# A hybrid attention and recurrence layer on one Trainium2 core: the two token tiles of a block share one matmul per level of the recurrence

## The chip, the core and the metric

The kernel runs on one core of a Trainium2 chip. A core has a matmul engine (TensorE, PE in the profile, with PEld its weight loads), a vector engine (VectorE, DVE), a scalar engine (ScalarE, ACT), GpSimd (POOL) and SyncE (SP), which issues the DMAs. SBUF is the on-chip memory of 128 partitions, PSUM the memory that matmuls write. Each engine works through its own queue in order, and they wait for each other at semaphores. The metric is the time of one execution on the device in microseconds; lower is better.

## What is computed

One layer for 2048 tokens of width 1024, all in 32-bit floats. The part that the change touches is the token mixer: differential attention (four heads, chunk-causal with chunks of 64 tokens) beside a gated recurrence (four heads, key width 128).

```python
h = _rmsnorm(x, ln1_w[l])
proj = h @ w_in[l]
dq, dk, dv, hq, hf, hi, hg = jnp.split(proj, offs, axis=-1)
...
f = lb + (1.0 - lb) * jax.nn.sigmoid(f_logit.astype(f32))
log_f = jnp.log(f)
k = 1.0 - f
...
def step(state, xs):
    qc, kc, vc, gc = xs
    b = jnp.cumsum(gc, axis=-2)
    rel = jnp.where(causal[:, :, None],
                    b[:, :, :, None, :] - b[:, :, None, :, :], -jnp.inf)
    att = jnp.einsum('bhtk,bhsk,bhtsk->bhts', qc, kc, jnp.exp(rel))
    o = (jnp.einsum('bhts,bhsv->bhtv', att, vc)
         + jnp.einsum('bhtk,bhkv->bhtv', qc * jnp.exp(b), state))
...
x = x + jnp.concatenate([o_diff, o_hgrn], axis=-1) @ w_out[l]
x = x + _conv_ffn(_rmsnorm(x, ln2_w[l]), w_up[l], conv_w[l], conv_b[l], w_down[l])
```

## The kernel before

The program has four stages: the mixer, the out-projection, the up-projection of the feed-forward part and its down-projection. Stages keep their tiles in pools of their own, which are opened when a stage is set up and take the place of the pools of the stage before; a tile that lies where an older one lay waits until the older one has been read for the last time.

**The mixer.** An outer loop runs over four slices `s` (one head of each kind; `WA`, `WB`, `WC` are the weights of a slice, loaded and split into a high and a low part). Inside, a loop over eight blocks `b` of 256 tokens runs the steps of a string of letters (`ORDER`, line 860 and following): projections (`proj_a`, `proj_b`, `proj_c`), transposes, scores and softmax (`attn`), the weighted sum (`attn_o`), the recurrence (`hgrn`) and its output (`hgrn_o`). A block is two tiles of 128 tokens, `j` or `g` = 0 and 1. In the first slice `phase1` (line 210) also normalizes x, transposes it and writes `hT` to memory, for the later slices. The string is only the order of the program text: the scheduler of the programming layer places each engine's instructions, so that projection and score matmuls stand between the matmuls of the recurrence.

**The recurrence**, `hgrn` (line 422). The decay within a tile is built up over seven levels, h = 1, 2, 4 to 64. At a level the queries in the second half of each group of 2h tokens meet the keys in the first half. For each of the two tiles `g`, a matmul of all keys of the tile (128 - h columns of weights) against 64 columns of queries writes half of the tile `lt` (one PSUM buffer, shared with `op` and `sp` of `hgrn_o`); the entries that belong together are copied under the mask `lmask` into `att`. Then the queries `qP` and the keys `kS` are multiplied in place by the decay of their group, and the decays `T` are multiplied pairwise for the next level:

```python
for g in range(2):
    PE.matmul(lt[0:nk, g]..., lhsT=kS[:, g * P:g * P + nk], rhs=qv[:, g * ng:(g + 1) * ng, 1, :], ...)
for g in range(2):
    DVE.copy_predicated(out=att[g][0:nk]..., mask=lmask[0:nk, li]..., data=lt[0:nk, g]...)
DVE.tensor_tensor(out=qv[:, :, 1, :], ...)
DVE.tensor_tensor(out=kvw[:, :, 0, :], ...)
```

`hgrn_o` (line 452) multiplies `att` with the values, adds the part of the running state, normalizes and gates, and writes the rows of the tile to `o_d`. `lmask` and three `att` tiles lie in pools that stay open through all stages; they are made once in `load_rest`, on GpSimd.

**The out-projection** loads eight weight tiles `wo0` to `wo7`, casts each to its high part on ScalarE (line 532) and subtracts for the low part on GpSimd or VectorE (line 533). `load_o` reads a tile of `o_d` back, transposes it and splits it into `oT`; the matmuls `pjo` (lines 594 to 596) go through the eight weight tiles in turn, three passes each.

Of the kernel before, what the change touches and what calls it, by code (L numbers as in the profile page):

```python
# [8 lines left out]
F32 = mybir.dt.float32  # L9
F32R = mybir.dt.float32r  # L10
BF16 = mybir.dt.bfloat16
U8 = mybir.dt.uint8
# [13 lines left out]
TOP, FEW, SMALL, SMALL2 = 480, 192, 320, 192  # L26
# [14 lines left out]
class Rows:  # L41
# [16 lines left out]
    def small(self, shape, dt, **kw):  # L58
        return self.pool.tile(shape, dt, **kw)


@with_exitstack
def hymba_kernel(ctx, tc, x, ln1_w, w_in, q_norm_w, k_norm_w, lam_q1, lam_k1, lam_q2, lam_k2,
# [54 lines left out]
    lmask = few.tile([P, 7, 64], U8, name="lmask")  # L118
    NATT = 3
    atts = [cst.tile([P, P], F32, name=f"att{n}") for n in range(NATT)]  # L120

# [13 lines left out]
    def load_rest(tmp, tmq):  # L135
        lamv = tmp[:, 0:256].rearrange("p (n e) -> p n e", n=4)
        lbd = tmp[:, 256:268].rearrange("p (n e) -> p n e", n=3)
        lmf = tmq[:, 0:448].rearrange("p (l e) -> p l e", l=7)
# [27 lines left out]
        for li, h in enumerate(LEVELS):  # L166
            v = lmf[:, li, :].rearrange("p (n h) -> p n h", h=h)
            n = 64 // h
            for pat, base, mul in (([-2 * h, n], 0, 1), ([2 * h, n], h - 1, -1)):
                POOL.affine_select(out=v, in_=v, pattern=[pat, [0, h]], compare_op=ALU.is_ge,  # L170
                                   fill=0.0, base=base, channel_multiplier=mul)
        POOL.tensor_copy(out=lmask, in_=lmf)
        for a in atts:
            POOL.memset(a, 0.0)
# [10 lines left out]
    with ExitStack() as ms:  # L185
        wp = pool(ms, "wp", 1)
# [26 lines left out]
        def phase1(b):  # L213
# [17 lines left out]
            for d0 in range(0, ND, 2):  # L231
# [4 lines left out]
                for dd in range(2):  # L236
                    dt = d0 + dd
                    ACT.activation(out=hT[:, 0, dt, :], in_=tp[:, dd, :], func=AF.Copy, scale=ln1c[:, dt:dt + 1])
                    DVE.scalar_tensor_tensor(out=hT[:, 1, dt, :], in0=tp[:, dd, :], scalar=ln1c[:, dt:dt + 1],  # L239
                                             in1=hT[:, 0, dt, :].bitcast(F32), op0=ALU.mult, op1=ALU.subtract)  # L240
# [15 lines left out]
        for s in range(4):  # L256
# [82 lines left out]
            def attn(b, j):  # L339
# [9 lines left out]
                for si, (k0, k1) in enumerate(segs):  # L349
                    for c in range(2):  # L350
# [8 lines left out]
                        if last:  # L359
                            DVE.memset(sc[0:64, w - 64:w], -3.0e38)  # L360
# [61 lines left out]
            def hgrn(b):  # L422
# [4 lines left out]
                att = [atts[(2 * b + g) % NATT] for g in range(2)]  # L427
                for li, h in enumerate(LEVELS):
                    nb = BLK // (2 * h)
                    nk = P - h  # L430
                    lt = ps.tile([P, 2, 64], F32, name="lt", tag=HT, bufs=HB)
                    qv = qP.rearrange("p (n two h) -> p n two h", two=2, h=h)
                    kvw = kS.rearrange("p (n two h) -> p n two h", two=2, h=h)
                    for g in range(2):
                        ng = nb // 2
# [468 lines left out]
```

## Time and profile before

| | us |
|---|---|
| median of 3 runs | 2775.85 (2774.70 to 2777.01) |
| the profiled execution | 2776.42 |
| its span, first to last instruction | 2774.7 |
| TensorE busy in the span | 2676.6 (96%) |
| VectorE busy | 1904.0 (69%) |
| ScalarE busy | 1201.2 (43%) |
| GpSimd busy | 1074.5 (39%) |

The mixer takes the first 45% of the span; the out-projection follows to about 1400 us, the up-projection to about 2100, the down-projection to the end. How the rows further down are to be read: in the timeline the first number is the start in us, the second how long the instruction (or the xN like it, merged) took, then engine, line, operation, out<-in by the program's names and the shapes; in brackets stands the idle time of the engine before it and what ended it. Matmuls overlap, so what one takes from its engine is the distance to the start of the next. A 32-bit matmul is two passes and shows as two instructions. In the table by stretch there are, for each stretch, its length and the busy time (with the number of instructions) of PE, PEld, DVE, ACT and POOL, then the granted share of TensorE's clock, the DMA share and GB/s. In the groups by line and shape: line, engine, operation, names, shapes, count, then busy us and mean ns of one, then idle time before them. In the list of waits: engine and tile that waited, for whom, us in total, times, longest.

### The profile page before, as it was taken

How to read it: one execution, taken by the hardware profiler on the slowest of the kernel's cores; microseconds unless marked ns; L12 is line 12 of the kernel's file. 1: busy time of each engine (PE TensorE's matmuls, PEld its weight loads, DVE VectorE, ACT ScalarE, POOL GpSimd, SP SyncE). 2: the span in 40 equal slices, each digit the busy share in tenths (PEclk: the TensorE clock that was granted, in tenths of full speed). 3: DMA queues.
4: the chain of work that ended last, by engine and by line, in shares of the span. 5: the costliest groups of instructions: out<-in, count | busy, mean ns of one | idle time of the engine just before them, and what ended most of it. 6: DMA issues, size and time to landing. Idle time of an engine off the chain costs nothing. (4 is left out here: it accounts for less than half of the span.)

```text
span 2774.7 us, 42676 instructions
## 1 busy us (share of the span) xinstructions
PE 2676.6 (96%) x15298; PEld 2342.9 (84%) x15298; DVE 1904.0 (69%) x3987; ACT 1201.2 (43%) x2814; POOL 1074.5 (39%) x1153
## 2 busy tenths in 40 slices
PE   7999999999999999989999999999999998899999
PEld 6998999999999999978887888887888886687887
DVE  5677855676567656673328666668777778977787
ACT  4555543454345434443334443445334344434332
POOL 3332222222222222121325434433343346887775
PEclk9999999999999999999999999999999999999999
DMA  5222311131211311124764222225222234775754
GB/s 187 100 84 98 121 68 69 69 122 65 73 68 59 107 69 69 39 80 155 237 204 144 92 76 84 91 76 183 76 91 81 80 91 122 166 163 132 180 169 170
DMA packets 236627, 306.15 MB, mean 110 GB/s; under 512 B 15374, under 2 KB 202110, under 8 KB 232318
## 3 DMA queue, kind: packets, MB, share of 16 engines
q1 hardware_dynamic: 229502, 278.25, 30.3%
q0 software_dynamic: 6912, 25.17, 5.3%
q8 instruction: 121, 1.98, 0.3%
q14 instruction: 92, 0.75, 0.1%
HBM read 198.50 MB, written 104.86 MB: 109 GB/s over the span
## 5 line engine op out<-in xcount | busy, mean ns | idle before, releaser
L679 PE MATMUL q<-xT,WS 128*128 128x512 f32 x704 | 274.3, 390 | 2.8 <-DVE xT L612 2.7
L678 PE MATMUL q<-xT,WS 128*128 128x512 f32 x704 | 274.0, 389 | 2.5 <-ACT xT L611 2.5
L680 PE MATMUL q<-xT,WS 128*128 128x512 f32 x704 | 274.2, 389 | 0.0
L792 PE MATMUL pd<-TW,SG 128*128 128x512 f32 x616 | 245.4, 399 | 19.9 <-DVE acc L798 6.5
L794 PE MATMUL pd<-TW,SG 128*128 128x512 f32 x616 | 242.3, 394 | 3.3 <-DVE SG L612 3.3
L793 PE MATMUL pd<-TW,SG 128*128 128x512 f32 x616 | 243.6, 396 | 1.0 <-DVE TW L612 1.0
L611 ACT CAST WS<-st 128x512 fp32r<-128x512 f32 x176 | 108.5, 618 | 243.0 <-PE q L680 230.4
L678 PE MATMUL q<-xB,WS 128*128 128x512 f32 x528 | 206.8, 392 | 1.9 <-ACT xB L611 1.9
L679 PE MATMUL q<-xB,WS 128*128 128x512 f32 x528 | 207.0, 392 | 1.1 <-DVE xB L612 1.1
L680 PE MATMUL q<-xB,WS 128*128 128x512 f32 x528 | 206.8, 392 | 0.9 <-DVE WS L612 0.9
L373 ACT ACTIVATE p<-sc,nm 128x1024 f32<-128x1024 f32 (+4 forms) x192 | 165.7, 863 | 96.7 <-DVE nm L362 95.8
L612 POOL TENSOR_TENSOR WS<-st,WS 128x512 fp32r<-128x512 f32 x44 | 88.0, 1999 | 281.8 <-ACT WS L611 270.9
L362 DVE TENSOR_REDUCE nm<-sc 128x1 f32<-128x1024 f32 (+4 forms) x192 | 174.3, 908 | 18.4 <-PE sc L358 16.1
L252 PE MATMUL pj<-WA,hT 128*128 128x384 f32 x512 | 175.9, 344 | 2.8 <-DVE hT L239 2.8
L254 PE MATMUL pj<-WA,hT 128*128 128x384 f32 x512 | 174.9, 342 | 0.0
L253 PE MATMUL pj<-WA,hT 128*128 128x384 f32 x512 | 174.8, 341 | 0.0
L792 PEld LDWEIGHTS pd<-TW,SG 128*128 128x128 f32 x616 | 117.8, 191 | 49.9 <-DVE acc L798 7.8
L679 PEld LDWEIGHTS q<-xT,WS 128*128 128x128 f32 x704 | 132.1, 188 | 31.3 <-DVE xT L612 4.0
L678 PEld LDWEIGHTS q<-xT,WS 128*128 128x128 f32 x704 | 132.2, 188 | 30.4 <-ACT xT L611 3.0
L680 PEld LDWEIGHTS q<-xT,WS 128*128 128x128 f32 x704 | 132.2, 188 | 27.3
L611 ACT CAST WS<-rawu 128x512 fp32r<-128x512 f32 x132 | 82.2, 624 | 160.4 <-PE q L680 160.3
L252 PE MATMUL pjc<-hT,WC 128*128 128x256 f32 x512 | 149.5, 292 | 0.0
(412 smaller groups left out, 7906.5 us busy)
## 6 DMA issues: line engine op xcount, KB each, us to landing
hT<-hTd SPq DMA_DIRECT2D x24, 2048.0 KB, 8.6
rawu<-in_w_up_dram SPq DMA_DIRECT2D x176, 256.0 KB, 3.0
x2d<-acc POOLq DMA_DIRECT2D x48, 512.0 KB, 6.3
gd<-c SPq DMA_DIRECT2D x176, 128.0 KB, 1.9
G<-gd SPq DMA_DIRECT2D x24, 768.0 KB, 4.3
xt<-in_x_dram SPq DMA_DIRECT2D x32, 512.0 KB, 4.1
hTd<-hT SPq DMA_DIRECT2D x8, 2048.0 KB, 7.8
rawd<-in_w_down_dram SPq DMA_DIRECT2D x22, 512.0 KB, 4.2
```

Of the source, the lines that this page charges most:

```text
L252: PE.matmul(dst, lhsT=lh, rhs=rh, start=dt == 0, stop=False)
L253: PE.matmul(dst, lhsT=lh, rhs=rl, start=False, stop=False)
L254: PE.matmul(dst, lhsT=ll, rhs=rh, start=False, stop=dt == ND - 1)
L362: DVE.tensor_reduce(out=nm, in_=sc[:, 0:w], axis=AX.X, op=ALU.max, negate=True)
L373: ACT.activation(out=p[:, 0:w], in_=sc[:, 0:w], func=AF.Exp, bias=nm, accum_out=l)
L611: ACT.copy(dst[:, 0], src)
L678: PE.matmul(dst, lhsT=w[:, 0, cs], rhs=b_[:, 0, dt], start=dt == 0, stop=False)
L679: PE.matmul(dst, lhsT=w[:, 0, cs], rhs=b_[:, 1, dt], start=False, stop=False)
L680: PE.matmul(dst, lhsT=w[:, 1, cs], rhs=b_[:, 0, dt], start=False, stop=dt == 3)
L792: PE.matmul(pd, lhsT=Sx[n][:, 0, k], rhs=w[:, 0], start=k == 0, stop=False)
L793: PE.matmul(pd, lhsT=Sx[n][:, 0, k], rhs=w[:, 1], start=False, stop=False)
L794: PE.matmul(pd, lhsT=Sx[n][:, 1, k], rhs=w[:, 0], start=False, stop=k == len(qs) - 1)
```

## The change

Both tiles of a block now share one matmul per level. For that the second tile of each block, the odd one, is kept in reversed token order through the whole mixer: `phase1` writes its columns of `hT` backwards, so its rows of scores, values and outputs are reversed as well. The mask of the last chunk in `attn` stands elsewhere for it, and `load_o` reverses it again on its way to the out-projection. With the order reversed, the queries of the first tile's second halves and of the second tile's first halves lie in one regular pattern (helper `view`). Per level ScalarE copies the 64 keys of each tile that are needed into a tile `kp` of 128 columns (two buffers); one matmul of `kp` against the 128 query columns of both tiles writes `lt`; of the four quarters the two that mix tiles are left unread by the masks. `lmask` now has a set for each tile, and there are two `att` tiles for each `g`. These tiles move from the pools that stay open into a pool `mc`, the first that the mixer opens; the next stage opens its pool of `wo` tiles first, on the same side.

```diff
-TOP, FEW, SMALL, SMALL2 = 480, 192, 320, 192
+TOP, FEW, SMALL, SMALL2 = 480, 128, 320, 192

...
+def view(a, off, *dims):
+    return bass.AP(a.tensor, a.offset + off, [list(a.ap[0])] + [list(d) for d in dims if d[1] > 1])
...
-    lmask = few.tile([P, 7, 64], U8, name="lmask")
-    NATT = 3
-    atts = [cst.tile([P, P], F32, name=f"att{n}") for n in range(NATT)]

...
         POOL.memset(lmf, 1.0)
-        for li, h in enumerate(LEVELS):
-            v = lmf[:, li, :].rearrange("p (n h) -> p n h", h=h)
-            n = 64 // h
-            for pat, base, mul in (([-2 * h, n], 0, 1), ([2 * h, n], h - 1, -1)):
-                POOL.affine_select(out=v, in_=v, pattern=[pat, [0, h]], compare_op=ALU.is_ge,
-                                   fill=0.0, base=base, channel_multiplier=mul)
-        POOL.tensor_copy(out=lmask, in_=lmf)
-        for a in atts:
+        for g in range(2):
+            for li, h in enumerate(LEVELS):
+                v = lmf[:, g, li, :].rearrange("p (n h) -> p n h", h=h)
+                n = 64 // h
+                for pat, base, mul in (([-2 * h, n], -g * h, 1), ([2 * h, n], h - 1 + g * h, -1)):
+                    POOL.affine_select(out=v, in_=v, pattern=[pat, [0, h]], compare_op=ALU.is_ge,
+                                       fill=0.0, base=base, channel_multiplier=mul)
+        POOL.tensor_copy(out=lmask[:, :, 0:7], in_=lmf)
+        for a in atts[0] + atts[1]:
...
     with ExitStack() as ms:
+        mc = pool(ms, "mc", 1)
+        lmask = mc.tile([P, 2, 8, 64], U8, name="lmask")
+        atts = [[mc.tile([P, P], F32, name=f"att{g}{n}") for n in range(2)] for g in range(2)]
         wp = pool(ms, "wp", 1)
         kv = pool(ms, "kv", KVB, side="right")
         pb = pool(ms, "pb", PBB, side="right")
...
                 for dd in range(2):
                     dt = d0 + dd
-                    ACT.activation(out=hT[:, 0, dt, :], in_=tp[:, dd, :], func=AF.Copy, scale=ln1c[:, dt:dt + 1])
-                    DVE.scalar_tensor_tensor(out=hT[:, 1, dt, :], in0=tp[:, dd, :], scalar=ln1c[:, dt:dt + 1],
-                                             in1=hT[:, 0, dt, :].bitcast(F32), op0=ALU.mult, op1=ALU.subtract)
+                    for j in range(2):
+                        js = slice(j * P, (j + 1) * P)
+                        src = tp[:, dd, js][:, ::-1] if j else tp[:, dd, js]
+                        ACT.activation(out=hT[:, 0, dt, js], in_=src, func=AF.Copy, scale=ln1c[:, dt:dt + 1])
+                        DVE.scalar_tensor_tensor(out=hT[:, 1, dt, js], in0=src, scalar=ln1c[:, dt:dt + 1],
+                                                 in1=hT[:, 0, dt, js].bitcast(F32), op0=ALU.mult, op1=ALU.subtract)
             dma(out=hT_d[b], in_=hT.bitcast(F32))
...
                         if last:
-                            DVE.memset(sc[0:64, w - 64:w], -3.0e38)
+                            if j:
+                                DVE.memset(sc[64:P, w - P:w - 64], -3.0e38)
+                            else:
+                                DVE.memset(sc[0:64, w - 64:w], -3.0e38)
...
                 T = f
                 TT = wk.tile([P, BLK], F32, name="TT", tag="TT", bufs=FB)
                 to = 0
-                att = [atts[(2 * b + g) % NATT] for g in range(2)]
+                att = [atts[g][b % 2] for g in range(2)]
                 for li, h in enumerate(LEVELS):
-                    nb = BLK // (2 * h)
-                    nk = P - h
+                    n, m = 64 // h, P // h
+                    qv = view(qP, h, (P - h, 2), (2 * h, n), (1, h))
+                    kl = view(kS, 0, (2 * h, n), (P + h, 2), (1, h))
+                    kf = view(kS, 0, (P + h, 2), (2 * h, n), (1, h))
                     lt = ps.tile([P, 2, 64], F32, name="lt", tag=HT, bufs=HB)
-                    qv = qP.rearrange("p (n two h) -> p n two h", two=2, h=h)
-                    kvw = kS.rearrange("p (n two h) -> p n two h", two=2, h=h)
-                    for g in range(2):
-                        ng = nb // 2
-                        PE.matmul(lt[0:nk, g].rearrange("p (n h) -> p n h", h=h), lhsT=kS[:, g * P:g * P + nk],
-                                  rhs=qv[:, g * ng:(g + 1) * ng, 1, :], start=True, stop=True)
+                    kp = wk.tile([P, P], F32, name="kp", tag="kp", bufs=2)
+                    ACT.copy(view(kp, 0, (2 * h, n), (h, 2), (1, h)), kl)
+                    PE.matmul(view(lt, 0, (64, 2), (h, n), (1, h)), lhsT=kp, rhs=qv, start=True, stop=True)
                     for g in range(2):
                         DVE.copy_predicated(
-                            out=att[g][0:nk].rearrange("p (n two h) -> p n two h", two=2, h=h)[:, :, 1, :],
-                            mask=lmask[0:nk, li].rearrange("p (n h) -> p n h", h=h),
-                            data=lt[0:nk, g].rearrange("p (n h) -> p n h", h=h))
-                    Tv = T.rearrange("p (n two) -> p n two", two=2)
-                    DVE.tensor_tensor(out=qv[:, :, 1, :], in0=qv[:, :, 1, :], in1=Tv[:, :, 0:1].broadcast_to([P, nb, h]), op=ALU.mult)
-                    DVE.tensor_tensor(out=kvw[:, :, 0, :], in0=kvw[:, :, 0, :], in1=Tv[:, :, 1:2].broadcast_to([P, nb, h]), op=ALU.mult)
-                    Tn = TT[:, to:to + nb]
-                    DVE.tensor_tensor(out=Tn, in0=Tv[:, :, 0], in1=Tv[:, :, 1], op=ALU.mult)
+                            out=att[g].rearrange("p (n two h) -> p n two h", two=2, h=h)[:, :, 1 - g, :],
+                            mask=lmask[:, g, li].rearrange("p (n h) -> p n h", h=h),
+                            data=lt[:, g].rearrange("p (n h) -> p n h", h=h))
+                    DVE.tensor_tensor(out=qv, in0=qv, in1=view(T, 0, (m + 1, 2), (2, n), (0, h)), op=ALU.mult)
+                    DVE.tensor_tensor(out=kf, in0=kf, in1=view(T, 1, (m - 1, 2), (2, n), (0, h)), op=ALU.mult)
+                    Tn = TT[:, to:to + m]
+                    DVE.tensor_tensor(out=Tn, in0=view(T, 0, (2, m)), in1=view(T, 1, (2, m)), op=ALU.mult)
                     T = Tn
-                    to += nb
+                    to += m
                 HG[b] = (qk, kS, qP, T)
 
             def hgrn_o(b):
                 qk, kS, qP, T = HG.pop(b)
-                att = [atts[(2 * b + g) % NATT] for g in range(2)]
...
                 for q in range(4):
                     kt = hf * 4 + q
                     PE.transpose(tp[:, q * P:(q + 1) * P], ot[:, kt * P:(kt + 1) * P], ident)
-                cs = slice(hf * 512, hf * 512 + 512)
-                ACT.copy(oT[0][:, cs], tp)
-                DVE.tensor_tensor(out=oT[1][:, cs], in0=tp, in1=oT[0][:, cs].bitcast(F32), op=ALU.subtract)
+                tv, (oh, ol) = tp.rearrange("p (q c) -> p q c", c=P), [
+                    t[:, hf * 512:hf * 512 + 512].rearrange("p (q c) -> p q c", c=P) for t in oT]
+                if i % 2:
+                    tv = tv[:, :, ::-1]
+                ACT.copy(oh, tv)
+                DVE.tensor_tensor(out=ol, in0=tv, in1=oh.bitcast(F32), op=ALU.subtract)
```

**Between two levels, on TensorE.** Slice 1, block 4, from the third to the fourth level (`tpa` transposes softmax weights, `sc` are scores, `pjc` is a projection). Before:

```order
L436 MATMUL lt<-qP,kS 124x64 x2
L406 MATMUL tpa<-ident,p 128x128 x3
L357 MATMUL sc<-kst,qT 128x256
L358 MATMUL sc<-kst,qT 128x256
L252 MATMUL pjc<-hT,WC 128x256
L253 MATMUL pjc<-hT,WC 128x256
L254 MATMUL pjc<-hT,WC 128x256
L252 MATMUL pjc<-hT,WC 128x256
L436 MATMUL lt<-qP,kS 120x64 x2
```

The same place in the changed kernel:

```order
L448 MATMUL lt<-qP,kp 128x128
L418 MATMUL tpa<-ident,p 128x128 x4
L366 MATMUL sc<-kst,qT 128x256
L367 MATMUL sc<-kst,qT 128x256
L261 MATMUL pjc<-hT,WC 128x256
L448 MATMUL lt<-qP,kp 128x128
```

One matmul stands for two, and between the levels there are one transpose more and three projection passes fewer.

**The copies, on ScalarE.** Slice 1, block 7, during the recurrence (`p` are the exponentials of the softmax, `qr`, `vst`, `qn` belong to the next projection). In the changed kernel:

```order
L385 ACTIVATE p,l<-sc,nm 128x1024
L447 COPY kp<-kS 128x128
L292 COPY qr<-pj 128x256
L293 COPY vst<-pj 128x128
L295 ACTIVATE qn<-qr 128x4x64
L447 COPY kp<-kS 128x128
L379 ACTIVATE wv<-nm,nm_8438 128x1
L385 ACTIVATE p,l<-sc,nm_8438 128x896
L447 COPY kp<-kS 128x128 x2
```

Before, no copy stands there; here two of the levels' copies stand right behind an exponential.

**The end of the mixer, on TensorE.** The last block of the last slice (`pjo` is the out-projection). Before:

```order
L472 MATMUL sp<-ig,kt__15922 128x128
L436 MATMUL lt<-qP,kS 127x64 x2
L436 MATMUL lt<-qP,kS 126x64 x2
L357 MATMUL sc<-kst,qT 128x512
L358 MATMUL sc<-kst,qT 128x512
L357 MATMUL sc<-kst,qT 128x384
L358 MATMUL sc<-kst,qT 128x384
L436 MATMUL lt<-qP,kS 124x64 x2
L594 MATMUL pjo<-wo_16310,oT 128x512
```

The first out-projection matmul in the changed kernel:

```order
L470 MATMUL op<-ones,qk 128x1
L471 MATMUL op<-ident,kS 128x128
L472 MATMUL op<-ig,att_185 128x128
L423 MATMUL av<-vst,aT 128x128 x7
L474 MATMUL op<-st,qP 128x128
L607 MATMUL pjo<-wo_16682,oT 128x512 x2
```

It stood among the levels of the last block, and now stands behind the last matmul that reads an `att` tile. The casts of the weights on ScalarE moved with it; the first of them now names a wait for TensorE:

```order
1597 L420 COPY aT_16499<-tpa_16494 128x512 [waits PE_49]
1598 L385 ACTIVATE p_16373,l_16374<-sc_16366,nm_16371 128x1024 [waits DVE_49]
1599 L420 COPY aT_16511<-tpa_16506 128x512 [waits PE_49]
1600 L420 COPY aT_16521<-tpa_16517 128x384 [waits PE_49,Activation_49]
1601 L542 CAST wo0_16682<-raw_16680 128x1024 [waits PE_49]
```

Before, this cast waited for nothing new and stood behind the activation of the last block's `pjc`.

## Rows read from the trace of the kernel before

**Rows 1.** Busy time by stretch: first slice, and a later slice.
```profile
50.00:340.00 290.00, 280.99 (x2062) 265.73 (x2062) 208.69 (x672) 154.56 (x430) 80.90 (x142) 0.99 0.30 107
340.00:640.00 300.00, 294.59 (x2168) 278.12 (x2167) 199.90 (x652) 135.89 (x398) 73.58 (x129) 1.00 0.22 76
```

**Rows 2.** Timeline of PE, slice 1, block 7: four levels, each with its successor.
```profile
619.97 0.66 PE L436 MATMUL lt<-qP,kS 128*127 128x64 f32 x4 [0.16 <-DVE st L477]
620.43 0.42 PE L254 MATMUL pj<-WA,hT 128*128 128x384 f32 x1
...
624.57 0.54 PE L436 MATMUL lt<-qP,kS 128*124 128x64 f32 x4
624.92 0.42 PE L253 MATMUL pj<-WA,hT 128*128 128x384 f32 x1
...
632.09 0.47 PE L436 MATMUL lt<-qP,kS 128*96 128x64 f32 x4
632.37 0.36 PE L254 MATMUL pj<-WB,hT 128*128 128x256 f32 x1
...
634.07 0.45 PE L436 MATMUL lt<-qP,kS 128*64 128x64 f32 x4
634.45 0.38 PE L253 MATMUL pj<-WB,hT 128*128 128x256 f32 x1
```

**Rows 3.** Timeline of PE, shortly before: sixteen passes of 128 columns.
```profile
613.71 2.05 PE L411 MATMUL av<-vst,aT 128*128 128x128 f32 x16
615.60 0.82 PE L406 MATMUL tpa<-ident,p 128*128 128x128 f32 x6
```

**Rows 4.** Waits in the mixer, those of the levels for kS.
```profile
PEld lt L436 <- DVE kS L445: 13.5, 23, 3.5
...
PE lt L436 <- DVE kS L445: 7.4, 15, 3.3
```

**Rows 5.** Timeline of ACT: an exponential and a copy of 128x128.
```profile
614.03 1.13 ACT L373 ACTIVATE p<-sc,nm 128x1024 f32<-128x1024 f32 x1
...
617.25 0.27 ACT L468 COPY kt__8142<-op 128x128 f32<-128x128 f32 x1
```

**Rows 6.** Groups by line and shape: DVE, 256 and 128 columns out of PSUM.
```profile
L239 DVE SCALAR_TENSOR_TENSOR hT<-tpx,ln1c,hT 128x256 fp32r<-128x256 f32 x64 | 29.4, 479 | 3.5 <-ACT hT L238 2.5
...
L470 DVE SCALAR_TENSOR_TENSOR o<-ig,dk,op 128x128 f32<-128x128 f32 x64 | 22.0, 343 | 3.7 <-ACT kt__16261 L468 0.7 <-ACT kt__8142 L468 0.5 <-ACT kt__12032 L468 0.5
```

**Rows 7.** Timeline at the start: masks and next work on POOL, and its reader.
```profile
17.98 6.32 POOL L170 TENSOR_SCALAR_AFFINE_SELECT tmq<-tmq 128x64 f32<-128x64 f32 x14
24.37 0.56 POOL L172 CAST lmask<-tmq 128x448 uint8<-128x448 f32 x1
28.89 0.19 POOL L98 TENSOR_SCALAR rq_m<-ssq 128x4 f32<-128x4 f32 x1 [3.97 <-DVE ssq L288]
...
30.28 1.04 POOL L290 TENSOR_TENSOR qn<-qr,rq_r 128x512 f32<-128x512 f32 x1
...
35.22 0.60 PE L300 MATMUL tpq<-ident,qn 128*128 128x128 f32 x4
```

**Rows 8.** Timeline at the mixer's end: PE, ACT and POOL.
```profile
1204.97 0.28 PE L254 MATMUL pjc<-hT,WC 128*128 128x256 f32 x1
...
1205.57 1.04 ACT L532 CAST wo<-raw 128x1024 fp32r<-128x1024 f32 x1
...
1206.68 2.38 POOL L533 TENSOR_TENSOR wo<-raw,wo 128x1024 fp32r<-128x1024 f32 x1 [6.89 <-ACT wo L532]
...
1230.44 0.71 PE L594 MATMUL pjo<-wo,oT 128*128 128x512 f32 x1
...
1232.15 0.39 PE L594 MATMUL pjo<-wo,oT 128*128 128x512 f32 x1
1232.38 0.39 PE L595 MATMUL pjo<-wo,oT 128*128 128x512 f32 x1
...
1256.96 0.39 PE L462 MATMUL op<-ig,att 128*128 128x128 f32 x2
```

More of the change, by code (lines that the diff above doesn't have):

```diff
@@ L137, in load_rest @@
         lbd = tmp[:, 256:268].rearrange("p (n e) -> p n e", n=3)
-        lmf = tmq[:, 0:448].rearrange("p (l e) -> p l e", l=7)
+        lmf = tmq[:, 0:896].rearrange("p (g l e) -> p g l e", g=2, l=7)
         for hf in range(2):
@@ L453, in hgrn_o @@
                 qk, kS, qP, T = HG.pop(b)
-                att = [atts[(2 * b + g) % NATT] for g in range(2)]
+                att = [atts[g][b % 2] for g in range(2)]
                 for g in range(2):
```

## The prediction

> **What bounds the kernel now.** I read the busy time by stretch first: in a slice of the mixer TensorE is busy 294.59 of 300 us, VectorE 199.90 and ScalarE 135.89 [rows 1]. So in the mixer, the first 45% of the span, the end is set by what TensorE has in its queue, plus its few waits; the other engines count where they make it wait or where they leave it without work. Then the timeline of TensorE over one recurrence: seven levels, each with four passes (two tiles, two passes each for 32-bit operands) [rows 2]. What a level takes from TensorE is read from its own start to the start of the next instruction, since the printed durations overlap. The first level goes from 619.97 to 620.43, 0.46 us; the third takes 0.35, the sixth 0.28, the seventh 0.38; of the others two repeat the first (0.46, 0.44) and one is 0.32. Sum 2.69, so 0.384 us a level. There are 7 levels x 8 blocks x 4 slices = 224, or 86 us of TensorE.
>
> **What one matmul for both tiles saves.** 64 columns are little for a pass: four of them take as long as the 128-wide passes of the attention, of which sixteen go from 613.71 to 615.60, 0.118 us each [rows 3]. The changed level has two passes of 128 columns, so 0.236 us at that price. 0.384 - 0.236 = 0.148; times 224 = 33.2 us less on TensorE.
> What the trace does not show is a 128-column pass whose moving columns lie apart (at the first level every second element, in two stretches). The upper bound: such a pass costs as much as the two 64-column passes that it replaces, which were read with the same step; the saving is then 0. The lower end is 0.236 a level. The first level (step of two elements) and the second and fourth cost 0.44 to 0.46, the last, whose columns are contiguous, 0.38, and it is the waiting levels that are dear, not those with a step: the third has steps too and takes 0.35. I take 0.236, the nearest row, and keep 0 for the range.
>
> **The wait in front of a level.** Before, the next level waits for three things on VectorE: two predicated copies, the update of qP, the update of kS. TensorE's waits for kS sum to 7.4 us, those of its weight loads to 13.5 us, over the whole mixer [rows 4]. Now kS is copied on ScalarE to kp (two buffers) and its update runs a level or more ahead, so TensorE waits for the qP update and finds kp made. That shortens the chain by one VectorE instruction. The order, however, puts the levels nearer together: between the first and second level of the block shown stood twelve projection passes, and now stand four and four score passes. The two cancel as far as I can read: 0, with a bound of 7.4 us of gain and as much loss.
>
> **What is added on ScalarE.** 224 copies of 128x128. A copy of that size takes 0.27 us [rows 5]: 60.5 us, about 15 a slice, which takes ScalarE from 135.89 to 151 of 300 us. It lies beside TensorE. Its price is what it delays behind it in ScalarE's queue: the exponentials on which the single score buffer waits. From 0 to 0.27 us for perhaps one copy in ten (6 us); I take 2.
> At the first level the copy reads elements of the two tiles in turn, 129 elements apart. [...] No row here has such a read; were those 32 copies twice as long, ScalarE would have 32 x 0.27 = 8.6 us more, and the sum would be the same, since the first copy of a block is made well before its matmul.
>
> **The reversed tile.** Writing hT is split by tile: 64 instructions of 256 columns become 128 of 128 on ScalarE and on VectorE, all in the first slice. VectorE is the busier of the two there, so the price goes by it: busy time per instruction was 29.4/64 = 0.459, and is 22.0/64 = 0.344 for the nearest row of 128 columns [rows 6]. So VectorE gets 64 x (2 x 0.344 - 0.459) = 14.7 us. Of these an eighth belongs to the first block, which has no TensorE work to hide under: 1.8 us on the path. The other 12.9 lie under a slice in which VectorE is busy 208.69 of 290 [rows 1]; bounds 0 and 12.9, I take 2, as TensorE has projections and scores there to go on with. No row shows a source read backwards: bounds, 0 and another doubling of the reversed half (64 x 0.344 = 22 us on VectorE, mostly hidden, so up to 4 on the path); I take 0. [...] In load_o the counts stay; the masking memset too.
>
> **Masks.** POOL makes two sets: 14 more selects, 6.32 us, and about 1 us for the larger memset and cast [rows 7]. It then ends near 32.3 instead of 24.9, and its next work, which began at 28.89, moves by 3.4 us; its product qn was there at 31.32 and is needed at 35.22. It just fits: 0, bound 3.
>
> **The end of the mixer.** Here the edit moves more than it says. lmask and the att tiles now are the first tiles of the mixer's own pools, on the place where the next stage puts its first weights, wo0. The order shows it: before, the first out-projection matmul stands among the last block's levels; now it stands behind the last matmul that reads att, and the ScalarE cast of wo0 waits for TensorE. Before, from the last projection pass (1204.97) to that att matmul (1256.96) 52 us pass, and 48 out-projection passes of 0.23 us, 11 us, fill TensorE's gaps from 1230.44 on [rows 8]. Now these come afterwards, behind a cast of 1.04 us and a POOL subtraction of 2.38. If the chain to the att matmul stayed 52 us long, the loss would be 11 + 3.4 = 14.5 us. But the chain gets shorter too: eight casts of about 1.04 us, and the VectorE halves of wo, stood in it in front of exponentials and copies, and a level's chain is shorter. If that gives back all, the loss is 0; a gain beyond it is excluded, as TensorE's work there shrinks by the levels alone, which are counted. I take 4, nearer to the short end, since ScalarE and VectorE with their queues set those 52 us: TensorE needs gaps there into which 11 us of other work fit.
>
> **Sum.** -33.2 + 0 + 2 + 1.8 + 2 + 0 + 4 = -23.4 us. The profiled execution took 2776.42 (span 2774.7); the median of the runs, 2775.85, is 0.6 lower, within their spread. Some 2752.5; I say 2752.
>
> **The rivals.**
> (1) The end of the mixer costs all it can: 14.5 instead of 4, so -13, 2763. For it: the order. Against it: what I said on the chain.
> (2) TensorE is freed, but VectorE or ScalarE chains bind in the blocks: two thirds of the 33 us come back as waits, so about 2775, no change. Against it: 67% and 45% busy, and so few waits now.
> (3) Slower: the copies stand in ScalarE's single queue among exponentials of 1.13 us [rows 5]. If a level finds its kp behind such a one, TensorE stands for up to 1.13 us. It decides from 23.4/1.13 = 21 such meetings among 224; with one a block, 32, it costs 36 us: 2789. For it: in the order a copy does stand right behind an exponential at several levels. Against it: two buffers of kp, so a copy is due a level early.
> (4) The strided pass costs what it replaces: saving 0, sum +10, 2786. Against it: the third level's 0.35.
> (5) All small costs vanish and the waits shrink: -33 to -40, near 2740.
>
> **How the numbers follow.** Forecast (2744 to 2760) 0.56; (1) 0.15; (2) 0.09; (3) 0.05; (4) 0.04; (5) 0.11. The range from 2737 to 2769 holds the forecast, (1), most of (5) and a part of (2). A measurement of this kernel can tell about 0.2%, 5.6 us, from no change. Faster by more than that: forecast, (5), (1) and a part of (2), 0.84; the rest of (2) 0.07 as the same; (3) and (4) 0.09 slower.
>
> **What would show it.** TensorE's passes into lt fall from 896 to 448, with a level at 0.23 to 0.26 us from start to next start; ScalarE gets 224 rows of about 0.27 us; the slices two and three shrink by 7 to 8 us each; the first out-projection matmul comes after the last matmul that reads att. Wrong would be: a level above 0.3 us, waits of TensorE for kp or qP of over 20 us in sum, or a stretch from the last projection pass to full TensorE that is more than 10 us longer than before.

## The result, and the profile after the change

The changed kernel takes 2799.97 us, median of four executions (2797.75 to 2802.42); the kernel before, run beside it, 2776.15. The ratio is 1.0086, with a 95% interval from 1.007 to 1.0102: **slower by 24 us**, where I had forecast 2752. The profiled executions are those with a span of 2774.7 us before and 2800.7 after; the accounts below are made between these two, 26 us apart.

First the whole program: span and mean granted clock of TensorE, before and then after.
```profile
core 0: 2774.7 us, clock 0.992
```
```profile
core 0: 2800.7 us, clock 0.981
```
The span gives no place, so I cut it where it can be compared: at TensorE's first pass into `lt` in a slice's first block (slices 0 to 3; in two expectations below "slice 4" is slice 3), at that of the last block but one, and at the last out-projection matmul. All from TensorE's timeline, in us, start to start:

| stretch | before | after | difference |
|---|---|---|---|
| start to slice 0's first level | 47.2 | 50.8 | +3.5 |
| slice 0 | 329.0 | 354.7 | +25.7 |
| slice 1 | 298.0 | 292.1 | -5.9 |
| slice 2 | 298.7 | 291.6 | -7.1 |
| slice 3, up to the last block but one | 212.6 | 206.6 | -6.0 |
| from there to the last out-projection matmul | 269.5 | 283.8 | +14.3 |
| the rest | 1319.7 | 1321.2 | +1.5 |

So the saving is there in every later slice, and two places lose more than all of it. The busy time of these stretches says how (columns: stretch, length, then busy time and count of TensorE matmul, weight load, VectorE, ScalarE, POOL; granted clock; DMA share; GB/s). Slices 0 and 1, before:
```profile
47.00:376.00 329.00, 318.66 (x2337) 301.51 (x2338) 229.70 (x733) 172.92 (x483) 88.59 (x158) 0.99 0.29 102
376.00:674.00 298.00, 292.31 (x2152) 276.06 (x2151) 198.17 (x648) 134.72 (x393) 73.37 (x129) 1.00 0.22 77
```
The same, and the two stretches of [rows 1], after:
```profile
51.00:405.00 354.00, 327.07 (x2222) 305.22 (x2222) 235.86 (x789) 193.39 (x593) 87.64 (x158) 0.95 0.27 94
405.00:698.00 293.00, 284.51 (x2048) 267.51 (x2048) 198.93 (x651) 148.54 (x451) 74.41 (x129) 1.00 0.23 78
50.00:340.00 290.00, 263.85 (x1773) 246.06 (x1774) 195.41 (x670) 161.61 (x502) 71.72 (x130) 0.94 0.26 95
340.00:640.00 300.00, 292.73 (x2105) 274.83 (x2104) 203.24 (x663) 154.18 (x465) 75.92 (x130) 1.00 0.24 82
```
Slice 1 is as planned: some 100 passes fewer, 7.8 us less busy, 2.8 us more idle. Slice 0 has 115 passes fewer and is busy 8.4 us *longer*, at a granted clock of 0.95 instead of 0.99, and its idle time goes from 10.3 to 26.9 us. Two losses, then: TensorE waits, and what it does is slower.

**What came as forecast.** Two levels with their successors, as in [rows 2], the groups of all levels and of the copies to `kp`, and TensorE's waits in front of a level:
```profile
645.18 0.39 PE L448 MATMUL lt<-qP,kp 128*128 128x128 f32 x2
645.32 0.43 PE L262 MATMUL pj<-WA,hT 128*128 128x384 f32 x1
...
651.43 0.46 PE L448 MATMUL lt<-qP,kp 128*128 128x128 f32 x2
651.64 0.42 PE L263 MATMUL pj<-WA,hT 128*128 128x384 f32 x1
```
```profile
L448 PE MATMUL lt<-qP,kp 128*128 128x128 f32 x448 | 96.0, 296 | 14.9 <-DVE qP L454 4.6 <-DVE st L487 4.4 <-ACT wv L379 3.6
L447 ACT COPY kp<-kS 128x128 f32<-128x128 f32 x224 | 69.8, 312 | 56.5 <-PE lt L448 46.4 <-DVE kS L455 5.8 <-DVE kst L316 2.0
```
```profile
PE lt L448 <- DVE qP L454: 4.6, 6, 2.1
...
PE lt L448 <- ACT kp L447: 1.7, 2, 1.4
```
448 passes for 896; from a level's start to the next start 0.14 to 0.21 us in these rows, and 53.0 us over the 224 levels of the trace, 0.236 a level. Counted the same way, the levels of the kernel before take 86.5 us. A copy takes 0.31 us.

**Where slice 0 slows.** TensorE's timeline at the change from the first block's projections to the second block's transpositions, after:
```profile
50.77 0.49 PE L448 MATMUL lt<-qP,kp 128*128 128x128 f32 x2 [1.44 <-ACT kp L447]
...
53.09 0.63 PE L241 MATMUL tpx<-ident,ht 128*128 128x128 f32 x4 [1.09 <-DVE hT L248]
54.53 0.39 PE L366 MATMUL sc<-kst,qT 128*128 128x256 f32 x1 [0.81 <-ACT p L385]
...
57.81 0.58 PE L366 MATMUL sc<-kst,qT 128*128 128x256 f32 x1 [0.91 <-ACT p L385]
...
59.32 0.52 PE L263 MATMUL pj<-WA,hT 128*128 128x384 f32 x1
59.64 0.52 PE L261 MATMUL pj<-WA,hT 128*128 128x384 f32 x1
...
62.20 0.33 PE L261 MATMUL pj<-WA,hT 128*128 128x384 f32 x1
62.37 0.33 PE L262 MATMUL pj<-WA,hT 128*128 128x384 f32 x1
```
Four gaps of 0.8 to 1.4 us, ended by VectorE or ScalarE. After the third of them the granted clock is 0.50, from 55.0 to 61.8 us, where projection passes start 0.32 us apart; right behind that, at 1.00, they start 0.17 apart. It is 0.50 again from 75.5 us on for 3.4 us, from 92.5 for 10.3, from 133.5 for 6.8 and from 174.4 for 6.9; from 50 to 100 us the granted clock is 0.82, and 0.97 before.

**Where the mixer's end loses.** What answers to [rows 8] (PE, ACT, POOL), with two instructions of VectorE:
```profile
1213.78 0.28 PE L263 MATMUL pjc<-hT,WC 128*128 128x256 f32 x1
...
1253.16 0.39 PE L472 MATMUL op<-ig,att 128*128 128x128 f32 x2
1255.20 0.70 PE L607 MATMUL pjo<-wo,oT 128*128 128x512 f32 x2
1257.15 0.50 PE L608 MATMUL pjo<-wo,oT 128*128 128x512 f32 x1 [1.26 <-POOL wo L543]
```
```profile
1253.60 1.06 ACT L542 CAST wo<-raw 128x1024 fp32r<-128x1024 f32 x1
```
```profile
1254.74 2.36 POOL L543 TENSOR_TENSOR wo<-raw,wo 128x1024 fp32r<-128x1024 f32 x1 [7.85 <-ACT wo L542]
```
```profile
1233.37 0.75 DVE L408 TENSOR_SCALAR p<-p,wv 128x1024 f32<-128x1024 f32 x1
...
1254.89 2.76 DVE L408 TENSOR_SCALAR p<-p,wv 128x1024 f32<-128x1024 f32 x1 [1.11 <-ACT wv L379]
```
The cast of `wo0` stood at 1205.57; now it stands right behind the last matmul that reads `att`. Then all eight pieces of `wo` are made one after the other while out-projection matmuls already wait for them. The chain to that matmul did become shorter, 39.4 us from the last projection pass instead of 52.0, but it was not the only thing that waited: from that matmul to the last out-projection matmul it now takes 226 us, before 198.

### The profile page after: what moved, and what is told of

Its sections match the earlier page's. It is cut to its first block, busy times and chain, and to the rows that moved or that the text cites. A ratio compares the mean times of both kernels' runs of the same rounds, so it can differ in the third digit from the quotient of the medians.

```text
span 2800.7 us, 42280 instructions
## 1 busy us (share of the span) xinstructions
PE 2671.6 (95%) x14850; PEld 2328.1 (83%) x14850; DVE 1903.7 (68%) x4051; ACT 1264.2 (45%) x3102; POOL 1085.1 (39%) x1168
## 5 line engine op out<-in xcount | busy, mean ns | idle before, releaser
L261 PE MATMUL pj<-WA,hT 128*128 128x384 f32 x512 | 178.9, 349 | 4.4 <-DVE hT L248 4.4
L263 PE MATMUL pj<-WA,hT 128*128 128x384 f32 x512 | 177.1, 346 | 0.0
L262 PE MATMUL pj<-WA,hT 128*128 128x384 f32 x512 | 176.8, 345 | 0.0
L423 PE MATMUL av<-vst,aT 128*128 128x128 f32 x1088 | 149.4, 281 | 1.2 <-ACT aT L420 1.1
```

The costliest lines, as they stand in the source:

```text
L261: PE.matmul(dst, lhsT=lh, rhs=rh, start=dt == 0, stop=False)
L262: PE.matmul(dst, lhsT=lh, rhs=rl, start=False, stop=False)
L263: PE.matmul(dst, lhsT=ll, rhs=rh, start=False, stop=dt == ND - 1)
```

## The experiments

Times are medians; "against before" is the ratio to the kernel before on the same chip.

**1. att tiles held for the whole program** (`after_att_kept`).
```
-        atts = [[mc.tile([P, P], F32, name=f"att{g}{n}") for n in range(2)] for g in range(2)]
+    atts = [[cst.tile([P, P], F32, name=f"att{g}{n}") for n in range(2)] for g in range(2)]   # top of the kernel
```


> The changed kernel with one thing undone: the four att tiles are held for the whole program again (as the three of before were), only lmask stays in the mixer's own pool. Theory A (end of the mixer): out-projection work cannot begin before the last matmul that reads att, because wo0 lies on the att tiles; TensorE then has gaps, and its clock falls. The first out-projection matmul stood at 1230.4 us before and at 1255.2 after; undone, it should stand near 1232, and the time should fall from 2800 by some 22 us to about 2778. Rival: the end is late for another reason (the reversed source in front of the out-projection, kp copies in the last block), then it stays at 2800 within 4.


2790.27 us (1.0047 [1.0032, 1.0062] against before): 10 us come back, not 22. The first out-projection matmul stands at 1240.5. Slice 0 is as slow as in the changed kernel (level 1 of slice 1 at 405). The place of `att` is a cause, and not the only one at this end.

**2. hT in one piece, the reversal moved into the transposition** (`after_whole_hT`): the transposition's moving matrix is a reversed identity for the odd tile, and L247 and L248 are the two instructions of before.
```
+        POOL.affine_select(out=jdent, in_=jdent, pattern=[[1, P]], compare_op=ALU.not_equal,
+                           fill=1.0, base=1 - P, channel_multiplier=1)
-  PE.transpose(tp[:, dd, j * P:(j + 1) * P], hts[j][...], ident)
+  PE.transpose(tp[:, dd, j * P:(j + 1) * P], hts[j][...], jdent if j else ident)
```


> The changed kernel with another thing undone: hT is again written by instructions of 256 columns. The odd tile is reversed by its transposition instead, whose moving matrix is a reversed identity, so that no operand has a negative step. Theory B (first slice): the split made TensorE wait for hT in the first slice, and the waits made its clock fall; undone, level 1 of slice 1 starts near 376 us as before, not at 405, and the time falls by 29 us to about 2771. Rival: the kp copies in ScalarE's queue cause the loss in the first slice; then nothing is won, 2800 within 5.


2770.64 us (0.9977 [0.9967, 0.9987]): 29 us back, as theory B said, and the kernel is now a little faster than before. Level 1 of slice 1 stands at 376. Slice 0:
```profile
47.00:376.00 329.00, 312.96 (x2224) 294.73 (x2225) 229.85 (x733) 184.53 (x539) 90.04 (x158) 0.98 0.29 102
```
Busy 5.7 us less than before, idle 5.7 us more: in this slice alone what a level saves comes back as waits.

**3. The split alone, on the kernel before** (`before_split`), all forward; and **its ScalarE half alone** (`before_split_act`).
```
-  ACT.activation(out=hT[:, 0, dt, :], in_=tp[:, dd, :], ...)          # and VectorE's likewise
+  for j in range(2):
+      ACT.activation(out=hT[:, 0, dt, js], in_=tp[:, dd, js], ...)    # and VectorE's likewise
```


> The kernel before with one part of the change alone: hT written tile by tile (128 instructions of 128 columns on ScalarE and on VectorE for 64 of 256), all forward. Theory B with the split as its cause: 2776 + 25 to 30, about 2803. If it is the backward read that costs: 2776 + 2 to 4 for the first block. If the kp copies are the cause: the same 2778.

> The kernel before with half of the split: ScalarE writes the high part of hT tile by tile (128 instructions of 128 columns), VectorE the low part by 256 columns as before. The whole split cost 31.5 us. If it is the number of instructions in either queue that costs, about half comes back, 2776 + 10 to 18. If VectorE's queue alone makes TensorE wait, 2776 + 0 to 4; if ScalarE's alone, 2776 + 25 to 32.


2807.62 us (1.0111 [1.0096, 1.0126]), 31.5 us more than before, from the split without reversal or `kp`; and 2791.37 (1.0047 [1.0033, 1.0061]), 13.5 more, for the half. Slice 0 of the one and of the other:
```profile
50.00:409.00 359.00, 336.08 (x2339) 315.27 (x2339) 235.56 (x790) 182.09 (x539) 89.32 (x158) 0.94 0.26 93
```
```profile
48.00:388.00 340.00, 322.79 (x2338) 304.21 (x2338) 230.02 (x733) 177.89 (x537) 90.03 (x158) 0.98 0.28 98
```
With the passes of before (2339 and 2337) the slice takes 30 us more: 12.6 us more idle (22.9 instead of 10.3) and 17.4 us more busy, at a clock of 0.94. An estimate from these rows: 0.06 of 359 us against 0.01 of 329 is 18 us of full speed lost, so the lower clock can account for all of the slower work. The half has 6.9 and 4.1. The split alone accounts for the loss in slice 0. By its expectation the half points to the number of instructions in either queue; experiment 5 tests that.

**4. The backward read** (`after_forward_read`).
```
-  src = tp[:, dd, js][:, ::-1] if j else tp[:, dd, js]
+  src = tp[:, dd, js]
```


> The changed kernel, still writing hT tile by tile, but reading PSUM forward for the odd tile too, so that the odd tile's tokens stay in order where the recurrence wants them reversed: this part of the result is left wrong, the instructions and their sizes are the same. If the backward read costs what I took (nothing), it stays at 2800 within 4; at my bound of 22 us more on VectorE and the same on ScalarE in the first slice, now that this slice is short of slack, it falls by 5 to 15 us.


2796.97 us (1.0068 [1.0054, 1.0082]), 3 us below the changed kernel, within the expected 4; the two intervals overlap. The instructions themselves, in the changed kernel and then here:
```profile
L247 ACT ACTIVATE hT<-tpx,ln1c 128x128 fp32r<-128x128 f32 x128 | 43.5, 369 | 19.5 <-DVE hT L248 12.6 <-PE tpx L241 6.2
L248 DVE SCALAR_TENSOR_TENSOR hT<-tpx,ln1c,hT 128x128 fp32r<-128x128 f32 x128 | 41.2, 345 | 5.0 <-ACT hT L247 4.0
```
```profile
L247 ACT ACTIVATE hT<-tpx,ln1c 128x128 fp32r<-128x128 f32 x128 | 43.5, 369 | 19.1 <-DVE hT L248 11.9 <-PE tpx L241 6.4
L248 DVE SCALAR_TENSOR_TENSOR hT<-tpx,ln1c,hT 128x128 fp32r<-128x128 f32 x128 | 41.2, 345 | 5.4 <-ACT hT L247 4.2
```
The same to the tenth of a us in sum: the backward read lengthens neither engine's instructions.

**5. Why the split costs so much: the turns** (`after_order`, `before_order`, `all_kept_order`). The row of L247 above names a suspect: ScalarE waits 12.6 us for VectorE's part of hT. The row of the kernel before, and TensorE's transpositions into `tpx`, before and after:
```profile
L238 ACT ACTIVATE hT<-tpx,ln1c 128x256 fp32r<-128x256 f32 x64 | 28.9, 473 | 11.3 <-PE tpx L235 7.0 <-DVE hT L239 4.0
L235 PE MATMUL tpx<-ident,ht 128*128 128x128 f32 x128 | 22.4, 301 | 16.5 <-DVE ht L229 8.4 <-DVE hT L239 6.4 <-DVE fo L418 1.6
```
```profile
L241 PE MATMUL tpx<-ident,ht 128*128 128x128 f32 x128 | 23.5, 313 | 22.8 <-DVE hT L248 14.3 <-DVE ht L235 8.4
```
ScalarE's waits for VectorE go from 4.0 to 12.6 us, and TensorE's waits for a free `tpx` tile from 6.4 to 14.3. Each ScalarE instruction on a `tpx` tile is held until the VectorE instruction ahead of it on that tile is through: in the trace 96 of the 128 wait for VectorE, before 32 of 64, and the first of each tile waits for TensorE alone, although other parts of the same hT are still being written. So with the split there are four turns for a tile where there were two, and each turn waits for its place in two queues that have other work. The changed kernel's ScalarE, then its VectorE, in slice 0:
```profile
87.82 0.35 ACT L247 ACTIVATE hT<-tpx,ln1c 128x128 fp32r<-128x128 f32 x1
...
88.38 0.36 ACT L420 COPY aT<-tpa 128x256 f32<-128x256 f32 x1
...
88.68 0.28 ACT L478 COPY kt__1145<-op 128x128 f32<-128x128 f32 x1
88.84 0.39 ACT L247 ACTIVATE hT<-tpx,ln1c 128x128 fp32r<-128x128 f32 x1
```
```profile
88.29 0.34 DVE L248 SCALAR_TENSOR_TENSOR hT<-tpx,ln1c,hT 128x128 fp32r<-128x128 f32 x1
88.55 0.41 DVE L345 TENSOR_TENSOR qk<-pjc,kS 128x256 f32<-128x256 f32 x1
89.00 0.35 DVE L480 SCALAR_TENSOR_TENSOR o<-ig,dk,op 128x128 f32<-128x128 f32 x1
89.27 0.35 DVE L248 SCALAR_TENSOR_TENSOR hT<-tpx,ln1c,hT 128x128 fp32r<-128x128 f32 x1
```
From one ScalarE part to the next 1.02 us, for 0.35 us of work each. The edit keeps every instruction and only takes the turns away:
```
-  for dd in range(2):  for j in range(2):  ScalarE part;  VectorE part
+  for dd in range(2):  for j in range(2):  ScalarE part
+  for dd in range(2):  for j in range(2):  VectorE part
```


> The changed kernel with nothing taken out: the same instructions of 128 columns, but for each tpx tile first the four of ScalarE, then the four of VectorE, instead of by turns. By turns each ScalarE instruction waits for the VectorE instruction before it, since both read one PSUM tile and are kept in order there. Theory D: the split costs by the length of this chain (32 tpx tiles, four turns of some 0.8 us instead of two of some 1.0 us, so about 1 us a tile, 32 us); without the turns most of it comes back: 2772 to 2782. Rival: the number of instructions, 64 more on each engine, fills the queues (busy time +14.7 us each): 2795 to 2800.

> The kernel before with the same order alone: for each tpx tile the two instructions of ScalarE, then the two of VectorE. Theory D: here too a turn is taken away, ScalarE waits 4.0 us in the first slice for VectorE's part of hT, so 1 to 6 us are won: 2770 to 2775. Rival: nothing, 2776 within 2.

> As all_kept (2753.7), with the order of before_order. Theory D: 1 to 6 us less, 2748 to 2753. Rival: 2754 within 2.


2771.86 us (0.9982 [0.9973, 0.9991]) for the changed kernel: 28 us come back with the same instructions, nearly all of the 29 that the whole hT of experiment 2 gave. The number of instructions by itself is out as the cause. Slice 0 takes 329 us again in the trace. 2769.97 (0.9972 [0.9959, 0.9984]) for the kernel before: 7 us, so the turns cost it, too, and a little more than forecast; in its trace slice 0 is as long as before (329) and begins 3.6 us earlier. 2755.48 (0.9921 [0.9906, 0.9936]) for the best version of experiment 6 (2753.68): nothing there, so theory D's forecast fails for it and the rival's holds. In the trace of `after_order`, ScalarE no longer waits for VectorE, and the two take a tile one behind the other:
```profile
L247 ACT ACTIVATE hT<-tpx,ln1c 128x128 fp32r<-128x128 f32 x128 | 37.0, 381 | 9.2 <-PE tpx L241 9.1
```
```profile
55.02 1.14 ACT L247 ACTIVATE hT<-tpx,ln1c 128x128 fp32r<-128x128 f32 x4 [0.37 <-PE tpx L241]
56.20 1.12 DVE L253 SCALAR_TENSOR_TENSOR hT<-tpx,ln1c,hT 128x128 fp32r<-128x128 f32 x4 [0.22 <-ACT hT L247]
```
The time from the first ScalarE to the last VectorE instruction of a tile, mean over the 32 tiles (from their starts and ends in the traces): before 2.74 us, half split 3.18, split 4.79, changed kernel 4.87, `after_order` 2.43, `before_order` 1.95. For that long the tile's buffer is not free, and the block's projections are not ready. Slice 0 follows it upward (329, 340, 359 and 355 us for the first four), but below 2.7 us nothing more is won there (329 for both reordered kernels). The half split shows that turns are not all: it has the two turns of before and still costs 13.5 us, with more work on ScalarE in the same chain. What the time follows, then, is the length of this chain; the turns are the larger part of it in the full split.

**6. Both undone, and what is left** (`both_undone`: experiments 1 and 2 together; `both_kp_on_vector`: the copies to `kp` by `DVE.tensor_copy`; `all_kept`: `lmask`, too, held for the whole program).


> The changed kernel with the two parts undone together: att tiles held for the whole program, and hT written by instructions of 256 columns behind a reversing transposition. If the two losses lie in different stages (first slice, end of the mixer) they add up: 2800 - 29.3 - 9.7 = 2761, some 15 us faster than the kernel before. Rival: with the first slice shorter, the end of the mixer is late for another reason, so that the second part wins nothing: 2770.

> As both_undone, with the 224 copies kS to kp on VectorE instead of ScalarE. In the first slice the changed kernel with whole hT gains nothing (level 1 of slice 1 at 376 us, as before), though the levels there take some 8 us less. Theory C: the copies on ScalarE delay the exponentials that TensorE waits for; on VectorE they don't, and 4 to 8 us more are won: about 2755. Rival: VectorE, the busier of the two, lengthens its own chain (qP, kS, reductions): 2761 or up to 2775.

> As both_kp_on_vector, with lmask held for the whole program too (two tiles of 448 bytes, one on the place of a pad; the small tile ln1r moves into the mixer's pool to make room). Nothing that the last block still uses lies under wo0 any more. Theory A says that the rest of the loss at the end of the mixer is lmask's: from level 1 of the last block but one to the last out-projection matmul it took 269 us before and 272 in both_kp_on_vector; it should take 264 to 267, and the time fall from 2756.5 to about 2751. Rival: that rest comes from elsewhere, then it stays at 2756 within 3.


2759.61 us (0.9934 [0.992, 0.9948]): the two losses add up as expected. 2756.47 (0.9923 [0.991, 0.9937]) with `kp` on VectorE: 3 us, less than the intervals tell apart, and level 1 of slice 1 stands at 375 in both, so theory C is not borne out. 2753.68 (0.9917 [0.9903, 0.993]) with `lmask` held: another 3 us that the times alone do not settle, and that lie within the rival's bound. In the traces the stretch that theory A named went from 272 to 268 us (264 to 267 expected), and the casts of `wo` stand again right behind the last projection pass (the first at 1184.13, that pass at 1183.54), so the place under `wo0` is free again. The best version of the idea is 0.8% faster than the kernel before. Part of that is not the idea's: the kernel before gains 7 us by the order of experiment 5 alone. With that order in both, on one chip, it is 2755.48 against 2769.97, 14.5 us, less than half of the 33 that the levels save on TensorE.

**7. The single cause at the mixer's end, and its clock** (`before_mc`: in the kernel before, `lmask` and the three att tiles in a mixer-local pool; `before_mc_filler`, `all_kept_filler`: with matmuls that keep TensorE busy in the last block).
```
+        mc = pool(ms, "mc", 1)                                   # before_mc: lmask and atts come from here
+                    if s == 3 and b == NB - 1:                   # the fillers
+                        for _ in range(6):
+                            PE.matmul(lt.rearrange("p g e -> p (g e)"), lhsT=ident, rhs=ident, start=True, stop=True)
```


> The kernel before with one part of the change alone: lmask and the three att tiles in a pool that is opened and closed with the mixer, so that wo0 lies on them. Theory A: +20 to 25, about 2798. My forecast's own term: +4 to +14.5, so 2780 to 2790. Rival (the place does nothing): 2776.

> As before_mc, with the same filler in the last block of slice 4. before_mc took 13.7 us more than before; in the stretch from level 1 of the last block but one to the last out-projection matmul TensorE was busy for 8.3 us longer with the same number of matmuls (clock 0.95 instead of 0.98) and idle for 4.8 us longer. If the clock is a cause by itself, filler that keeps TensorE busy wins back some 4 to 8 us of the 13.7: 2782 to 2786. If it only accompanies the waits: 2790 or up to 2800.

> As all_kept, with six matmuls of identity by identity ahead of each level's matmul in the last block of slice 4 alone (42 of some 0.24 us, 10 us of TensorE work whose result is overwritten). They can stand in the gaps in which TensorE waits there for VectorE. [...]


2789.80 us (1.0047 [1.0031, 1.0064]) for `before_mc`: 13.7 us for the place alone, in my own range and below theory A. With filler 2793.40 (1.0056 [1.0041, 1.0071]), and 2760.16 (0.9942 [0.9929, 0.9954]) for `all_kept_filler`, where `all_kept` took 2753.68. From level 1 of the last block but one to the last out-projection matmul, before, `before_mc` and `before_mc_filler`, each from its own trace:
```profile
1186.00:1455.00 269.00, 255.13 (x1399) 217.16 (x1399) 116.50 (x231) 110.87 (x278) 65.23 (x82) 0.98 0.54 173
```
```profile
1186.00:1468.00 282.00, 263.38 (x1401) 223.05 (x1401) 119.73 (x231) 112.17 (x278) 65.44 (x82) 0.95 0.51 164
```
```profile
1184.00:1474.00 290.00, 272.13 (x1493) 231.41 (x1491) 117.23 (x233) 111.95 (x278) 68.49 (x83) 0.97 0.50 161
```
With the filler the clock was 0.97 instead of 0.95, and the stretch was longer by 8 us, about what TensorE is busy longer (8.75 us). So at this end nothing is won by keeping the clock up with such work. Whether the clock costs time there by itself is left open, since the filler changed both; so is its own share in slice 0, where 17.4 us of slower work and 12.6 us of idling came and went together.

## Why the prediction was wrong

- **The matmul** (-33.2): right. 0.236 us a level forecast, 0.236 measured, and 33.5 us less in the levels of the trace (86.5 to 53.0); slices 1 and 2 shrank by 5.9 and 7.1 us, where I had named 7 to 8 each. The strided moving columns cost nothing that shows, so rival (4) is out.
- **The wait in front of a level, and the copies** (0 and +2): nearly right. TensorE's waits for qP sum to 4.6 us and for `kp` to 1.7, far from the 20 that would have spoken against me; rival (3) is out. A copy takes 0.31 us, not 0.27. TensorE's idle time in a later slice grew by 1.9 to 2.8 us, so about +8 in all, where I said 2 and allowed 6. Experiment 6 did not show that the copies are the cause. The copy of the first level, whose elements lie 129 apart, and that of the second, on ScalarE in the changed kernel:
```profile
89.10 0.38 ACT L447 COPY kp<-kS 128x128 f32<-128x128 f32 x1
...
90.69 0.31 ACT L447 COPY kp<-kS 128x128 f32<-128x128 f32 x1
```
  Over all blocks the first takes 0.375 us on the mean, each of the other six 0.30. The doubling that I had allowed was an estimate that no run shows, and the 2.4 us in sum lie beside TensorE.
- **Masks** (0): no loss was found. With the longer masks but hT whole, level 1 of slice 0 stands at 47 as before. POOL's selects, 6.32 us in [rows 7], took 10.59:
```profile
18.44 10.59 POOL L173 TENSOR_SCALAR_AFFINE_SELECT tmq<-tmq 128x64 f32<-128x64 f32 x28
```
- **The split of hT** (+1.8 and +2, bounds 0 to 12.9): **the step that failed.** It cost 31.5 us by itself. In the changed kernel 3.5 us of the loss stand ahead of slice 0's first level, where I had 1.8; the rest, in slice 0, is what I had put at 2. I priced it by the busy time that it adds to the busier queue, got the 14.7 us about right (41.2 - 29.4 = 11.8 in the rows), and took that for an upper bound, hidden by TensorE's other work as VectorE was busy for only 208.69 of 290 us [rows 1]. But on a path through two queues that work adds to the path itself, and every hand-over adds its waits: a tile took 4.79 us with the split and 2.74 without. The row of [rows 6] showed one already: 2.5 us of VectorE's idle time ended by ScalarE's hT. I read only its duration. What I also left out: with the split, slice 0 lost more than the 12.6 us of waiting, as its passes took 17.4 us longer, too, at a granted clock of 0.94 (0.99 before).
  The row of L238 in experiment 5 showed the turns, too: in the kernel before, ScalarE waited 4.0 us for VectorE on tiles that both only read, in the changed kernel 12.6. By that row I should have counted turns on a tile, not busy time alone.
- **The mixer's end** (+4, bounds 0 to 14.5): the mechanism was right, the size wrong. The stretch grew by 14.3 us although its levels became cheaper; the place alone costs 13.7. The chain to the last att matmul became 12.6 us shorter, as I had hoped. It does so without a cheaper level, too: in `before_mc`, with the levels of before, it is 39.9 us, so the work that left the chain explains it. The term that was too small is what comes behind: 28.3 us more from that matmul to the last out-projection matmul, where I had counted 11 + 3.4 = 14.4. There stand the eight pieces of `wo`, which I had counted as one cast and one subtraction (3.4 us), and POOL's part of them next to VectorE's softmax: 2.76 us for an instruction that took 0.75 twenty us earlier.
  The 2.76 us began 0.15 us after a POOL subtraction of 2.36; the other 31 of these instructions in the trace took 0.73 to 0.76 us, none of them next to such a subtraction. What made this one long was not shown.
- **Rivals.** (1) was right in its place and price (14.5), but not enough. (2), the chains that bind, came true in slice 0 alone: with hT whole, its 5.7 us of saving are idle time there. Slower was to come from (3) or (4); it came from a term that I had not made a rival at all.

The sum by stretches, from the table: +3.5 + 25.7 - 5.9 - 7.1 - 6.0 + 14.3 + 1.5 = +26. With the two parts undone the idea gives 2759.6, and 2753.7 with `lmask` held and the copies on VectorE as well. That this is close to my 2752 is luck: I forecast it for a kernel that has both losses.

## What to carry to other kernels

Where two engines take turns on one tile, count the hand-overs, and let one engine finish before the other begins: the same instructions in another order gave back 28 us here, 7 in the kernel before, and nothing in the best version, where hT was whole already. An added instruction is hidden by other work only if nobody waits for the chain it stands in; the busy share of its engine alone did not tell that here. A tile that moves to another pool also moves under whatever is allocated on its place next: look for what then waits for its last reader, and for everything behind that.

## What the runs showed of the hardware

- A source read with a negative step took as long as a forward one: 369 and 345 ns for 128x128 from PSUM on ScalarE and VectorE, in the changed kernel and in `after_forward_read`. A transposition by a reversed identity reversed at no cost that shows: in `after_whole_hT` its passes took 298 ns on the mean, those by the plain identity 302.
- TensorE's granted clock fell to 0.50 after three gaps of 0.8 to 1.4 us among short passes, with a fourth while it was low, and projection passes then started 0.32 us apart instead of 0.17. In slice 0 with the split the same passes took 17.4 us longer in sum than before.
- Moving columns that lie apart cost a matmul next to nothing in the changed kernel: from the first pass of a level to its second it took at least 0.115 us at the first level, with a step of two elements, and 0.108 to 0.112 at the later ones.
